# A decoder layer on eight cores: an own buffer for V's last columns, an fp16 copy of w_down made in DRAM, and the first block sums ahead of the LayerNorm statistics

## The chip, the cores and the metric

The kernel runs on all 8 cores of one Trainium2 chip, each core on 2048 of 16384 tokens. The time is that of the slowest core, in microseconds (us) on the device. Each execution of such a program is in one of two states: fast, or slow, where the cores of one die (0 to 3 or 4 to 7), or of both, are granted a lower TensorE clock. The engines are PE (TensorE, matmuls), DVE (VectorE), ACT (ScalarE), POOL (GpSimd) and SP (SyncE, which here only issues transfers). DMA transfers are issued from POOL's queue (q0 in the profile, which can also cast) and from SP's (q1).

## The reference, cut to what matters

```python
proj = x @ w_in + b_in                       # q, k, v of two attention groups
y = concat(rms_norm(group A), rms_norm(group B)) @ w_out
x = layer_norm(ALPHA * x + y, ln1)
gate, up = split(x @ w_up)
x = layer_norm(ALPHA * x + (silu(gate) * up) @ w_down, ln2)   # 2048 -> 5632 -> 2048
```

## The kernel before: the parts that matter

A core first computes K and V for eight tiles of 512 tokens (its own four and the four before them, for the attention window), then attention, the output projection, and SwiGLU. SwiGLU runs twice (`st` = 0, 1: 1024 tokens each), each time with the hidden width in two halves (`g`), with seven block products in place of eight; the operands of the seven are "block sums" made on VectorE.

A scheduler records every operation with the buffers it reads and writes, and puts semaphore waits between them **in program order**. A DMA with `joins=` adds itself to a buffer's writers, and whoever reads the buffer waits for all writers recorded so far.

```python
    for kc in range(KC):                                       # 16 chunks: POOL's queue
        S_.dma("pool", s0[:, kc, :], k.xT_d[0, :, kc, :], [], [b_], ...)          # x, tile 0
        S_.dma("pool", wv[:, kc, 0:1024], k.wv_d[kc, :, 0:1024], [], [bwv[kc]], ...)
    S_.dma("sp", bv, k.bv_d, [bwv[11]], [bbv], "bv")
    load_x(1, (2, 2, 4, 4, 4))
    for h in range(8):
        S_.dma("pool", wk[h], k.wk_d[h], [], [bwk[h]], ...)
    for q in range(4):                                         # V's last 128 columns
        S_.dma("pool", wv[:, 4 * q:4 * q + 4, 1024:1152], ..., [], [], "wvb",
               joins=bwv[4 * q:4 * q + 4])
    ...
    for kc in range(KC):                                       # V of tile 0
        S_.pe(mm, [bx[0][kc], bwv[kc]], k.bBK)
    ...
    for t in range(2, 8):                                      # the other token tiles
        if t >= 3: kb_tile(t)
        for blk in range(4): v_tile(t, blk); flush()           # 2 output buffers, stored by SP
        for h in range(8): k_tile(t, h)                        # 3 output buffers, stored by SP
```

A V tile stores 128 rows of 2304 bytes (2048 in tiles 0 to 2), a K tile 128 rows of 1024 bytes. The down projection loads each block of w_down as fp32, cast to fp16 on the way, once for each `st`; between its blocks it stores and reloads partial results (`z2s`, `x1s`).

The softmax here doesn't subtract the row's maximum and nothing guards it: scores larger than these inputs give would overflow.

## Time and profile before

| | before |
|---|---|
| timed runs, at first | 3138.67 to 3421.52 us, median of 3: 3149.82 |
| profiled run | 2991.6 us, mean granted clock 0.98 on all cores |
| PE's first matmul / first K matmul | 92.83 / 155.56 us |
| token tiles 3 to 7 (267 to 573 us) | PE busy 304.9 of 306 us |
| PE idle in the four down projections | 41 us |

The page of before: busy time by engine, then busy tenths in 40 slices of the span, for PE and the DMA engines.

```profile
PE 2756.5 (92%) x14966; PEld 1324.0 (44%) x15077; DVE 1965.6 (66%) x2700; ACT 735.6 (25%) x1075; POOL 554.9 (19%) x579
...
PE   0799999999999799989999999997899999999995
...
DMA  9745311457665755869977745578588678544653
```

PE is the bound; only the places where its row is below 9 can be won. The first is the start. PE's timeline (start, duration, engine, line, operation, count, and the idle time before with what ended it):

```profile
92.83 30.73 PE L526 MATMUL sp<-arena 128*128 128x512 bf16 x126 [92.83 <-DMA arena<-wv]
126.40 29.32 PE L538 MATMUL sp<-arena 128*128 128x512 bf16 x125 [2.84 <-DVE arena L450]
155.56 4.70 PE L481 MATMUL sp<-arena 128*128 128x512 bf16 x21
```

L526 and L538 are V of tiles 0 and 1, L481 is K. The others show in the list of PE's waits (us in total, times, longest):

```profile
PE sp L526 <- DMA arena<-wv: 92.8, 1, 92.8
PE sp L1382 <- DVE arena L1555: 19.9, 8, 5.8
PE sp L1382 <- DVE arena L1557: 19.6, 6, 8.5
PE sp L1382 <- ACT arena L1510: 14.9, 2, 7.4
```

L1555 and L1557 add reloaded partial results in the down projection; L1510 stands in the first gate/up block of each `st`, behind two LayerNorm tiles on ACT. The stage windows (stretch, length, busy time of each engine, granted clock, DMA share, GB/s) for token tiles 3 to 7, the first down projection, and the second half's first block:

```profile
267.00:573.00 306.00, 304.90 (x1603) 158.55 (x1621) 155.17 (x229) 3.12 (x5) 4.54 (x9) 1.00 0.33 82
1556.00:1700.00 144.00, 133.98 (x610) 59.79 (x609) 83.65 (x106) 0.57 (x1) 4.24 (x8) 0.98 0.81 183
...
2110.00:2160.00 50.00, 40.82 (x174) 17.77 (x172) 33.59 (x41) 11.89 (x17) 10.96 (x10) 0.93 0.52 135
```

In the first row DMA is a third busy and PE has no gap. DMA issues (KB each, median us from issue to landing):

```profile
arena<-wdn POOLq DMA_DIRECT2D x32, 1408.0 KB, 14.7
z2s<-arena SPq DMA_DIRECT2D x48, 512.0 KB, 12.2
...
ka<-arena SPq DMA_DIRECT2D x64, 128.0 KB, 1.7
```

### The profile page before, as it was taken

The page shows a single profiled execution, that of the slowest core. Times are in us where ns is not written, and L with a number is a line of the kernel's source. Part 1 is how long each engine was busy: PE and PEld are TensorE (multiplying, and loading weights), DVE is VectorE, ACT ScalarE, POOL GpSimd, SP SyncE. Part 2 cuts the span into 40 slices and gives each one's busy share as a digit, 9 for nine tenths or more (in the row PEclk, how much of TensorE's full clock was granted, in tenths as well). Part 3 has the DMA queues.
Part 4 walks back from the last instruction along what each step waited for, and adds up shares of the span by engine and source line. Part 5 has one row for each costly group of instructions (what it writes and reads, how often), then busy time and mean ns, then how long its engine had stood idle before and what let it go on. Part 6 is the DMA issues. An engine that isn't in the chain of part 4 may idle for free.

```text
span 2990.6 us, 41458 instructions; the slowest of 8 cores (2976.1 to 2990.6 us)
## 1 busy us (share of the span) xinstructions
PE 2756.5 (92%) x14966; PEld 1324.0 (44%) x15077; DVE 1965.6 (66%) x2700; ACT 735.6 (25%) x1075; POOL 554.9 (19%) x579
## 2 busy tenths in 40 slices
PE   0799999999999799989999999997899999999995
PEld 0344555444566444434444444443344444444442
DVE  0164554588788754478865566675788756666787
ACT  0000000177665424523310022211233200122114
POOL 4000000022111174711100000035200000000167
PEclk9999999999999899999999999999999999999997
DMA  9745311457665755869977745578588678544653
GB/s 158 126 94 114 87 52 50 101 113 130 134 145 121 205 164 155 225 109 152 152 129 181 178 88 91 95 155 216 138 172 171 126 173 184 112 87 89 145 128 116
DMA packets 192570, 400.59 MB, mean 134 GB/s; under 512 B 89072, under 2 KB 112752, under 8 KB 174704
## 3 DMA queue, kind: packets, MB, share of 16 engines
q0 software_dynamic: 36032, 186.43, 38.1%
q1 hardware_dynamic: 142512, 186.32, 22.1%
q10 hardware_dynamic: 13824, 25.17, 2.7%
q8 instruction: 123, 2.02, 0.3%
q14 instruction: 79, 0.65, 0.1%
HBM read 491.42 MB, written 97.06 MB: 197 GB/s over the span
## 4 chain that ended last, share of the span: by engine, by line
PE 78%; DMA 7%; DVE 4%; another core or an unknown queue 3%; issue 3%; ACT 2%; SPq 1%; POOL 1%; ACTq 0%; DVEq 0%; POOLq 0%
PE sp L1382 47%; PE sp L481 7%; PE sp L728 7%; PE sp L468 6%; PE sp L1194 4%; DMA z2s<-arena 4%; SPq L139 1%; DMA arena<-x1s 1%; PE sp L526 1%; PE sp L538 1%; DMA arena<-z2s 1%; PE sp L770 1%; DVE arena L1288 1%; ACT arena L358 1%
## 5 line engine op out<-in xcount | busy, mean ns | idle before, releaser
L1382 PE MATMUL sp<-arena 128*128 128x512 f16 x7408 | 1615.4, 381 | 57.8 <-DVE arena L1555 19.9
L1382 PEld LDWEIGHTS sp<-arena 128*128 128x128 f16 x7408 | 726.3, 98 | 947.5 <-issue 86.5
L1475 DVE TENSOR_TENSOR arena<-sp,arena 128x512 f32<-128x512 f32 (+1 forms) x348 | 236.9, 689 | 175.3 <-PE sp L1382 154.9
L1557 DVE TENSOR_TENSOR arena<-arena,sp 128x512 f32<-128x512 f32 x256 | 166.7, 682 | 131.1 <-PE sp L1382 102.8
L1194 PE MATMUL sp<-arena 128*128 128x512 bf16 x1003 | 224.5, 384 | 10.0 <-DMA arena<-wob 6.9
L728 PE MATMUL sp<-arena 128*128 128x512 bf16 x976 | 226.9, 381 | 5.4 <-ACT arena L358 2.3
L450 DVE TENSOR_TENSOR arena<-sp,arena 128x384 bf16<-128x384 f32 (+1 forms) x81 | 47.8, 605 | 272.5 <-PE sp L526 111.3
L481 PE MATMUL sp<-arena 128*128 128x512 bf16 x1001 | 220.1, 379 | 1.2
L139 POOL DMA_DIRECT2D arena<-wup x88 | 47.0, 535 | 840.2 <-DVE arena L1395 576.7
L1403 DVE TENSOR_TENSOR arena<-arena 128x2048 f16<-128x2048 f16 (+1 forms) x118 | 191.3, 1621 | 0.0
L468 PE MATMUL sp<-arena 128*128 128x384 bf16 (+1 forms) x1036 | 182.4, 337 | 0.4
L1238 POOL TENSOR_TENSOR arena<-arena 128x512 f32<-128x512 f32 x120 | 168.4, 1403 | 25.0 <-ACT arena L1236 22.5
L1237 POOL TENSOR_TENSOR arena<-arena 128x512 f32<-128x512 f32 x120 | 159.1, 1326 | 56.1 <-DVE arena L1557 30.0
L358 ACT ACTIVATE arena<-sp,arena 128x512 bf16<-128x512 f32 (+1 forms) x37 | 24.7, 667 | 575.1 <-PE sp L501 499.8
L1194 PEld LDWEIGHTS sp<-arena 128*128 128x128 bf16 x1024 | 101.1, 99 | 134.0 <-issue 16.7
L1508 ACT ACTIVATE arena<-sp 128x512 f32<-128x512 f32 x86 | 51.4, 597 | 440.1 <-PE sp L1382 439.0
L1236 ACT ACTIVATE arena<-arena 128x512 f32<-128x512 f32 x120 | 75.6, 630 | 332.1 <-DVE arena L1557 170.9
L1395 DVE TENSOR_TENSOR arena<-arena 128x2048 f16<-128x2048 f16 (+1 forms) x118 | 156.3, 1324 | 0.7 <-DMA arena<-wdn 0.6
L1475 DVE TENSOR_TENSOR arena<-arena 128x512 f16<-128x512 f32 (+1 forms) x304 | 154.7, 567 | 0.0
L481 PEld LDWEIGHTS sp<-arena 128*128 128x128 bf16 x1024 | 100.2, 98 | 120.2
L728 PEld LDWEIGHTS sp<-arena 128*128 128x128 bf16 x1024 | 97.7, 98 | 116.2 <-issue 6.4
L468 PEld LDWEIGHTS sp<-arena 128*128 128x128 bf16 x1040 | 101.7, 98 | 79.6
(131 smaller groups left out, 2474.5 us busy)
## 6 DMA issues: line engine op xcount, KB each, us to landing
arena<-wup POOLq DMA_DIRECT2D x88, 1024.0 KB, 10.0
arena<-wdn POOLq DMA_DIRECT2D x32, 1408.0 KB, 14.7
z2s<-arena SPq DMA_DIRECT2D x48, 512.0 KB, 12.2
arena<-xres SPq DMA_DIRECT2D x32, 512.0 KB, 7.6
arena<-wob SPq DMA_DIRECT2D x32, 512.0 KB, 6.8
x1s<-arena ACTq DMA_DIRECT2D x64, 256.0 KB, 6.4
arena<-x1s SPq DMA_DIRECT2D x32, 512.0 KB, 7.3
arena<-z2s SPq DMA_DIRECT2D x32, 512.0 KB, 9.0
```

The costliest lines, as they stand in the source:

```text
L139: return self._add(q, lambda: eng.dma_start(out=out, in_=in_), reads, writes, joins, semkey=semkey)
L468: ins = nc.tensor.matmul(bank(k, bk)[:, 0:c1 - c0], x[:, kc, blk * 128:blk * 128 + 128], wv[:, kc, c0:c1], start=(kc == 0), stop=(kc == KC ...
L481: ins = nc.tensor.matmul(bank(k, bk), wk[h][:, kc, :], x[:, kc, :], start=(kc == 0), stop=(kc == KC - 1))
L728: ins = nc.tensor.matmul(bank(k, bk), w[:, kc, :], x[:, kc, :], start=(kc == 0), stop=(kc == KC - 1))
L1194: ins = nc.tensor.matmul(bank(k, bk), w[:, kc, :], y[:, kc, hh * 512:(hh + 1) * 512], start=(first and i == 0), stop=(last and i == len(kc ...
L1237: S_.pool(lambda: nc.gpsimd.tensor_tensor(out=za, in0=za, in1=z, op=ALU.add), [bz, bza], [bza])
L1238: S_.pool(lambda: nc.gpsimd.tensor_tensor(out=qa, in0=qa, in1=sq, op=ALU.add), [bsq, bqa], [bqa])
L1382: ins = nc.tensor.matmul(bank(k, bk), w, x, start=(first and i == 0), stop=(last and i == len(ws) - 1), skip_group_check=True)
L1395: S_.dve(lambda: nc.vector.tensor_tensor(out=v, in0=w[:, 0:n, :], in1=w[:, n:2 * n, :], op=ALU.add), [bw], [b])
L1403: S_.dve(lambda: nc.vector.tensor_tensor(out=v, in0=w[:, :, 0:128], in1=w[:, :, 128:256], op=ALU.subtract), [bw], [b])
L1475: S_.dve(lambda: nc.vector.tensor_tensor(out=o, in0=a, in1=b, op=op), [ba, bb], [bo])
L1557: S_.dve(lambda: nc.vector.tensor_tensor(out=v, in0=v, in1=o, op=op), [b, bo], [b])
```

## The change

Its intent has three parts. (a) V's last columns get their own buffer, so tile 0 need not wait for them. (b) While PE projects token tiles 3 to 6, 16 DMAs copy w_down to fp16 in DRAM, so that its 32 later loads read half the bytes and need no cast. (c) The sums for PE's next products are made before the statistics, and two LayerNorm tiles leave the first block.

```diff
+    bwvb = Buf("wvb")
@@
-               joins=bwv[4 * q:4 * q + 4])
+               joins=[bwvb])
@@ def v_tile
-            S_.pe(mm, bx[t] + bwv, [k.bBK[bk]])
+            S_.pe(mm, bx[t] + bwv + ([bwvb] if c1 > 1024 else []), [k.bBK[bk]])
@@ for t in range(2, 8)
         for h in range(8):
+            if 3 <= t < 7 and h % 2 == 0:
+                i = (t - 3) * 4 + h // 2
+                k.bwdh[i] = Buf("wdh%d" % i)
+                S_.dma("pool", k.wdh_d[i // 2, i % 2], k.wdn_d[i // 2, i % 2].rearrange("p a j m -> p (a j m)"), [], [k.bwdh[i]], "wdh")
             k_tile(t, h)
@@ loads of w_down: from k.wdh_d[p, g], after k.bwdh[...], in place of k.wdn_d[p, g]
@@ first gate/up block
                         if i == 1:
+                            x_sums(((G3, B21, B11, ALU.subtract),))
+                            u_sums(st, f + 1, "P")
                             while fins:
                                 fins.pop(0)()
...  (the other sums follow one by one)
-                    run_jobs(2)
-                    run_acts()
```

## The prediction

> **What bounds the kernel.** TensorE: the page gives PE 92% busy, and the chain of waits is 78% PE. Only PE's idle stretches can be won. Timeline, stage windows and PE's waits show three kinds:
>
> 1. Start: PE's first matmul (L526) starts at 92.83 us, released by a wv load. By the code, V's last-column loads join the buffers of V's main columns and precede the matmuls in program order, so the first matmul waits for a load queued behind x0, wv, x1 and wk. But bv, which waits for the twelfth wv chunk, was issued at 39.3 us, and ropeA, which waits for the end of x1, at 63.8: tile 0's operands are there near 50 us, tile 1's near 64.
> 2. Down projection: PE waits for VectorE, which waits for x1s/z2s reloads behind z2s stores. The windows show 134.0 of 144, 125.3 of 143, 134.1 of 144 and 134.5 of 138 us busy: 41 us idle, and some 2 us at half rate (0.43 us a matmul, not 0.22) after each gap over 5 us, as in the Trainium skill (TensorE: Matmul & The Clock Gate, What's actually happening). DMA share is 0.81 to 0.85 in the first three.
> 3. First gate/up block of each half: PE waits 0.92 and 1.74 us for VectorE L1395, then 7.43 and 7.45 us for ScalarE L1510, queued behind two LayerNorm tiles, then runs slowly for some 2 us.
>
> **What the change does.**
> (a) Tile 0 of V is paced by its loads and ends near 50 us, not 123. Not all 73 us are won: the V stores stand behind ropeA (63.8 us) on SP's queue and there are two V output buffers, so blocks 2 and 3 free their banks only near 75 us; tile 1's second half ends near 90, when wk has landed too. The first K matmul (L481) moves from 155.5 to about 91 us: 64 us won, all on the critical path, kept by the PE-bound rest.
> (b) Sixteen fp32-to-fp16 copies, 23 MB written. At the software queue's 163 GB/s (186.4 MB in 38.1% of the span; estimate) each takes 9 us of all engines: 140 to 190 us in one burst from about 205 us, where DMA share is 0.1 to 0.9. K stores (1.7 us) will slow to maybe 10; three output buffers and eight banks cover it: cost 0 to 8 us. Later the 32 wdn loads need half the read and no cast: 1.44 MB at q1's 282 GB/s (estimate) is 5 us, not 9, per 16.7 us block. Of 45 us (41 idle plus cold matmuls) I expect 24 back.
> (c) The first G3 and P sums precede the statistics, and no LayerNorm tile stands before L1508/L1510: 20 us in two halves.
>
> Sum: 64 + 24 + 20 - 4 = about 105 us.
>
> **The time.** Before's profiled run took 2991.6 us (fast state); its timed runs, 3138 to 3421, are slow by the 1.5% rule. The change should come to about 2886 in fast runs (ratio 0.965); timed like before, mostly slow, 3150 - 105 = about 3042. The range must hold both: 2870 to 3085. Faster by over 2%: 0.87; within 2%: 0.11; slower: 0.02.
>
> **What would show it.** First L526 before 15 us, first L481 at 85 to 100 us; PE without gaps from 100 to 500 us though DMA share is near 1 from 205 to about 380; w_down loads landing in under 10 us (14.7 before); PE's waits on L1555/L1557 falling from 39.5 to under 20 us; no 7.4 us wait on L1510.
>
> **What would make it wrong.** Copies to DRAM much slower than loads, stalling K and V stores or the x and wq loads; HBM shared by all cores setting the pace in the start; reload waits staying because store latency, not w_down, sets them; timed runs in another state than before's.

## The result, and the profile after

The change made the kernel slower. In the first measurement it took 3228.26 us (median of 4, 3223.96 to 3514.29) against 3145.28 for before (median of 4): ratio 1.0263, 95% interval 1.0218 to 1.0309. Ratios in this text are the mean time of one kernel's fast runs over that of the other's of the same rounds, so not quite the ratio of the medians. The predicted ratio was 0.965, and the measured time lies above the predicted range of 2870 to 3085 us.

That profile fell in the slow state (mean clock 0.90 to 0.93). The same kernel was therefore run again; in the call f2_after all four of its runs and all seven of before were fast, and the ratio was 1.0224 (1.0208 to 1.0239; medians 3062.63 and 2995.99). All lines of "after" are from that profile, taken in the same state as before's. Its page:

```profile
PE 2764.1 (90%) x15077; PEld 1323.3 (43%) x15077; DVE 1981.4 (65%) x2700; ACT 735.6 (24%) x1075; POOL 562.6 (18%) x595
...
PE   6895118999999989999999999999999999999995
...
DMA  9949993124576574476886675446867756554523
```

PE's zero at the start is gone, and so are the later 7s and 8s but one. But there is a new hole, "5118", from slice 4 on, and under it DMA is at 9. PE's timeline at the start (L529 is before's L526, L541 its L538, L484 its L481):

```profile
11.30 5.20 PE L529 MATMUL sp<-arena 128*128 128x512 bf16 x16 [11.30 <-DMA arena<-wv]
...
57.91 15.66 PE L541 MATMUL sp<-arena 128*128 128x512 bf16 x64 [2.91 <-DVE arena L453]
89.89 15.52 PE L541 MATMUL sp<-arena 128*128 128x512 bf16 x64 [16.32 <-DVE arena L453]
105.25 15.06 PE L484 MATMUL sp<-arena 128*128 128x512 bf16 x69
```

So part (a) works: K starts at 105 us, not 155.6. PE's waits:

```profile
PE sp L471 <- DVE arena L344: 134.1, 4, 76.2
PE sp L484 <- DVE arena L453: 31.7, 1, 31.7
...
PE sp L1389 <- DVE arena L1565: 8.5, 6, 3.3
...
PE sp L1389 <- DVE arena L1563: 3.4, 3, 1.5
```

The down projection's waits (L1563 and L1565, before's L1555 and L1557) fell from 39.5 to 11.9 us, and the ACT wait is gone. But PE now waits 166 us in the projections for VectorE to empty its banks. The window from tile 3's start shows how bad it is:

```profile
214.00:467.00 253.00, 87.54 (x411) 41.56 (x409) 33.27 (x50) 1.05 (x2) 11.67 (x23) 0.67 0.99 121
```

PE is busy 88 of 253 us. VectorE is not the cause: it is busy 33 us. Its timeline names what it waits for (L347 writes a K tile's output buffer):

```profile
391.11 0.69 DVE L347 TENSOR_TENSOR arena<-arena 128x512 bf16<-128x512 f32 x1 [84.11 <-DMA ka<-arena]
...
415.12 0.69 DVE L347 TENSOR_TENSOR arena<-arena 128x512 bf16<-128x512 f32 x1 [21.01 <-DMA ka<-arena]
...
441.02 0.69 DVE L347 TENSOR_TENSOR arena<-arena 128x512 bf16<-128x512 f32 x1 [22.90 <-DMA ka<-arena]
...
464.27 0.69 DVE L347 TENSOR_TENSOR arena<-arena 128x512 bf16<-128x512 f32 x1 [20.24 <-DMA ka<-arena]
```

One K store is done every 23 to 26 us, where PE makes a K tile every 3.45 us. The DMA view of the same stretch (225 to 430 us), packets and bytes by queue:

```profile
q0 software_dynamic: 1534, 22.67, 96.9%
q1 hardware_dynamic: 1533, 2.65, 4.4%
...
ka<-arena SPq DMA_DIRECT2D x5, 128.0 KB, 92.6
```

**1534 packets of POOL's queue (the copies, and until about 248 us the x loads ahead of them) and 1533 of SP's (the stores, and two loads of rotary tables between them).** Here the two queues take turns, one packet each; but the turns of POOL's queue take 97% of the engines' time and those of SP's 4%. Over the whole execution:

```profile
arena<-wdh POOLq DMA_DIRECT2D x32, 1408.0 KB, 8.2
z2s<-arena SPq DMA_DIRECT2D x48, 512.0 KB, 7.2
wdh<-wdn POOLq DMA_DIRECT2D x16, 1408.0 KB, 145.7
```

The later loads got what was intended (14.7 to 8.2 us, the z2s stores 12.2 to 7.2). The copies landed 46 to 241 us after issue: one queue, one burst. The first, issued at 218.5 us, landed 46.4 us later; the last, issued at 225.9 us, 241.3 us later. So one landed every 13.5 us ((467.2 - 264.9) / 15).

### The profile page after: what moved, and what is told of

It is laid out like the page before. It is cut to its first block, busy times and chain, and to the rows that moved or that the text cites. A ratio compares the mean times of both kernels' runs of the same rounds, so it can differ in the third digit from the quotient of the medians.

```text
span 3222.9 us, 41604 instructions; the slowest of 8 cores (3139.9 to 3222.9 us)
## 1 busy us (share of the span) xinstructions
PE 2952.4 (92%) x15077; PEld 1368.3 (42%) x15077; DVE 1987.2 (62%) x2700; ACT 735.5 (23%) x1075; POOL 557.1 (17%) x595
## 3 DMA queue, kind: packets, MB, share of 16 engines
q0 software_dynamic: 37312, 209.50, 36.5%
## 4 chain that ended last, share of the span: by engine, by line
PE 84%; another core or an unknown queue 6%; DMA 3%; DVE 2%; issue 2%; SPq 1%; ACT 1%; POOL 1%; DVEq 0%; ACTq 0%; POOLq 0%
PE sp L1389 54%; PE sp L1201 7%; PE sp L735 6%; PE sp L484 6%; PE sp L471 4%; DMA vs<-arena 1%; DMA arena<-xT 1%; SPq L139 1%; POOL arena L139 1%; PE sp L541 1%; PE sp L777 1%; DVE arena L1650 1%; ACT arena L359 0%; DMA ys<-arena 0%
## 5 line engine op out<-in xcount | busy, mean ns | idle before, releaser
L1389 PE MATMUL sp<-arena 128*128 128x512 f16 x7408 | 1783.2, 409 | 4.9 <-DVE arena L1565 1.9
L1389 PEld LDWEIGHTS sp<-arena 128*128 128x128 f16 x7408 | 767.1, 104 | 1021.3 <-issue 600.8
L471 PE MATMUL sp<-arena 128*128 128x384 bf16 (+1 forms) x1040 | 192.1, 348 | 134.0 <-DVE arena L344 133.6
L1565 DVE TENSOR_TENSOR arena<-arena,sp 128x512 f32<-128x512 f32 x256 | 167.6, 683 | 169.2 <-PE sp L1389 168.5
L484 PE MATMUL sp<-arena 128*128 128x512 bf16 x1024 | 224.0, 381 | 28.5 <-DVE arena L453 28.5
L1201 PE MATMUL sp<-arena 128*128 128x512 bf16 x1024 | 232.5, 392 | 2.3 <-DMA arena<-wob 2.3
L735 PE MATMUL sp<-arena 128*128 128x512 bf16 x1024 | 233.9, 381 | 0.0
L1410 DVE TENSOR_TENSOR arena<-arena 128x2048 f16<-128x2048 f16 (+1 forms) x118 | 202.2, 1713 | 0.0
L471 PEld LDWEIGHTS sp<-arena 128*128 128x128 bf16 x1040 | 104.1, 101 | 220.8 <-issue 145.2
L347 DVE TENSOR_TENSOR arena<-arena 128x512 bf16<-128x512 f32 x96 | 77.9, 812 | 181.4 <-DMA ka<-arena 168.8
L484 PEld LDWEIGHTS sp<-arena 128*128 128x128 bf16 x1024 | 100.5, 98 | 150.4 <-issue 31.6
L1201 PEld LDWEIGHTS sp<-arena 128*128 128x128 bf16 x1024 | 102.6, 100 | 132.5 <-issue 33.8
L1402 DVE TENSOR_TENSOR arena<-arena 128x2048 f16<-128x2048 f16 (+1 forms) x118 | 157.4, 1334 | 0.0
```

The lines of the kernel that those rows point to most:

```text
L471: ins = nc.tensor.matmul(bank(k, bk)[:, 0:c1 - c0], x[:, kc, blk * 128:blk * 128 + 128], wv[:, kc, c0:c1], start=(kc == 0), stop=(kc == KC ...
L484: ins = nc.tensor.matmul(bank(k, bk), wk[h][:, kc, :], x[:, kc, :], start=(kc == 0), stop=(kc == KC - 1))
L735: ins = nc.tensor.matmul(bank(k, bk), w[:, kc, :], x[:, kc, :], start=(kc == 0), stop=(kc == KC - 1))
L1201: ins = nc.tensor.matmul(bank(k, bk), w[:, kc, :], y[:, kc, hh * 512:(hh + 1) * 512], start=(first and i == 0), stop=(last and i == len(kc ...
L1389: ins = nc.tensor.matmul(bank(k, bk), w, x, start=(first and i == 0), stop=(last and i == len(ws) - 1), skip_group_check=True)
L1402: S_.dve(lambda: nc.vector.tensor_tensor(out=v, in0=w[:, 0:n, :], in1=w[:, n:2 * n, :], op=ALU.add), [bw], [b])
```

## The experiments

Theory A: the burst of copies starves the K and V stores, and the rest of the change works. Within it, A1: a store is held because each of its packets waits for one packet of a copy; A2: the copies use up the engines or the DRAM, whatever their packets. Rival B: the denser kernel is granted a lower clock, and that ate the gain.

| run | what it is | ratio to before (95%) | us against before | PE busy, 214 to 514 us |
|---|---|---|---|---|
| f2_after | the change | 1.0224 (1.0208 to 1.0239) | +67 | 132 of 300 |
| e1_no_copy | the change without the copies | 0.9751 (0.9734 to 0.9769) | -75 | 300 |
| e4_copy_only | the copies alone | 1.0451 (1.0426 to 1.0476) | +135 | other times |
| e2_short_runs | the change, copies in runs of 352 elements | 0.969 (0.9654 to 0.9725) | -93 | 300 |
| e5_half_rows | the change, copies in half rows | 0.9843 (0.9698 to 0.9988) | noisy | 223 |
| e3_paced | the change, copies spread | 0.9684 (0.9665 to 0.9703) | -95 | 288 |
| e8_paced_half | e3, in half rows | 0.9668 (0.9648 to 0.9689) | -99 | 289 |
| e9_more_v_out | e8, more V output buffers | 0.966 (0.964 to 0.968) | -102 | other times |
| e6b_own_buffer | part (a) alone | 0.9821 (0.9802 to 0.984) | -54 | - |
| e7_early_sums | part (c) alone | 0.9854 (0.9767 to 0.9942) | noisy | - |

"Us against before" is (ratio - 1) times the median of before: 2996.68 for e1 to e4, 2995.99 for f2, e6b, e8 and e9. The call with e5, e6, e7 and f1 was disturbed: of its 11 runs of before 8 were slow, and even the fast ones went from 3018.83 to 3046.79. There only the traces are used, not the ratios. e6 is not in the table: it has no ratio, and e6b repeats it. e1 to e4 ran on chip 7 and all later runs on chip 0 (f1's expectation below says the chip of the first four, which is not so); the medians of before, 2996.68 and 2995.99, agree.

### Taking the copies away, and the copies alone

e1 takes the copies out of the changed kernel; e4 puts them alone into the kernel before, as the change has them.

```diff
# e1, against the change
-                S_.dma("pool", k.wdh_d[i // 2, i % 2], k.wdn_d[i // 2, i % 2]..., [], [k.bwdh[i]], "wdh")
-  (("d", st, g, p), k.wdh_d[p, g]...)          # loads of w_down
+  (("d", st, g, p), k.wdn_d[p, g]...)
```

> The changed kernel with w_down's copy undone (own buffer for V's last columns and early block sums stay). Theory A (the burst of 16 DRAM-to-DRAM copies starves the K and V stores, so the projections stop; the rest of the change works): no PE gap over 5 us between 110 us and the end of the projections, where the changed kernel had 253 - 91 = 162 us idle from 214 to 467 us; first K matmul L484 near 103 us as there (155.5 before); down-projection waits as before (about 40 us); time ratio to before 0.970 to 0.982 (52 + 20 us of 3143 won). Rival B (the chip grants a lower clock as the kernel gets denser, and that ate the gain, not the copies): ratio 0.995 or more, with a mean clock below that of before's runs in the same rounds by about as much.

> The kernel before with the fp16 copy of w_down alone, issued in one burst as in the change. Theory A: PE idles 140 to 185 us in token tiles 3 to 5, the down projection gets back about 40 us, ratio to before 1.030 to 1.045. Rival B: the loss is not in the copies: ratio under 1.01.

The stage windows of e1 and of e4:

```profile
214.00:514.00 300.00, 300.00 (x1606) 156.21 (x1604) 150.57 (x222) 3.12 (x5) 4.78 (x9) 1.00 0.34 82
```

```profile
267.00:573.00 306.00, 137.81 (x659) 66.80 (x657) 63.22 (x96) 1.37 (x2) 10.68 (x22) 0.72 0.89 118
```

e1 won 75 us and PE had no gap from 214 to 514 us; e4 lost 135 us and PE was busy 137.8 of the 306 us from 267 to 573 us, where it was busy 304.9 before. Both are as theory A expected, e4's ratio at the upper edge of its range. B falls: e1's mean clock was 0.98, as before's, and it was faster. e4's mean clock was 0.96, but in that window, where PE stands idle, it was 0.72 against before's 1.00; 0.28 less for 306 of 3140 us makes 0.03, which covers the lower mean. The two parts add up: -75 + 135 = +60, against +67 measured for the whole, where each of the three has an interval of some 5 to 8 us.

The clock bears on one thing only: the first measurement's times lie 5% above the later ones. The change's two fast runs there had mean clocks of 0.90, against 0.96 in f2. Before's first timed runs have no recorded clock, so that they shared it is likely and not shown.

### Why the copies starve the stores: shorter runs

```diff
# e2, against the change: the same bytes in the same burst, in runs of 352 elements
-  S_.dma("pool", k.wdh_d[i // 2, i % 2], k.wdn_d[i // 2, i % 2].rearrange("p a j m -> p (a j m)"), ...)
+  S_.dma("pool", k.wdh_d[i // 2, i % 2].rearrange("p (c e) -> c p e", c=16),
+         k.wdn_d[i // 2, i % 2].rearrange("p a j m -> p (a j m)").rearrange("p (c e) -> c p e", c=16), ...)
```

> The changed kernel with each copy issued over runs of 352 elements (1408 bytes read, 704 written) in place of whole 5632-element rows; same bytes, same burst. Theory A1 (a store's eight 1 KB packets per DMA engine each wait for one packet of a copy, about 18 KB written or 2.4 us, so a K store takes 20 us): the copies' packets shrink to about 6 KB written (230 packets a copy, not 80), a K store in the burst takes 6 to 10 us instead of 20 and more, PE's idle time in the burst falls from 162 us to 20 to 70 us, ratio to before 0.975 to 1.0. Rival A2 (the DMA engines' or DRAM's rate is used up by the copies, whatever their packets): K stores stay at 20 us and more, idle stays at 140 us or more, ratio about 1.02.

The DMA view of e2 from 235 to 400 us, and its window from 214 to 514 us:

```profile
q0 software_dynamic: 18918, 14.97, 86.7%
q1 hardware_dynamic: 5981, 9.36, 20.2%
...
ka<-arena SPq DMA_DIRECT2D x23, 128.0 KB, 8.2
```

```profile
214.00:514.00 300.00, 300.00 (x1606) 156.34 (x1605) 150.13 (x222) 3.12 (x5) 21.24 (x25) 1.00 1.05 147
```

PE is full for 300 us with the DMA engines at a share of 1.05, more than in the change (0.99). Full DMA engines did not stop PE, so A2 falls. For A1 this run is support, not proof. One expectation was off: I thought that several runs would share a packet (230 packets a copy). The queue's totals give (69056 - 36032) / 16 = 2064 a copy, one for each of the 2048 runs and 16 more. And the counts are not one for one here: 18918 to 5981, though SP's queue had more than one transfer in flight on average (23 K stores of 8.2 us and nine V stores of 9.3 us make 272 us in these 165 us). By turns of one such packet a K store would be held about 1.3 us (165 us x 16 engines / 18918, nine times); it took 8.2 us. The expected 6 to 10 us had been worked out from 230 packets, so that hit was luck, or the engine's turns hold several of the packets that the profile counts; no run here tells which.

Two things keep e2 from being the best form. The copies ran slower (POOL was held between issues, and the last copy was issued at 406.7 us, not 225.9), and DMA stayed full to about 530 us. So the wq loads behind the copies came late, and PE lost 14 us at the start of attention. Besides, e2 changes the pace of issue along with the packets, though its queue stayed deep: seven copies were issued by 226 us, and each later one 0.3 us after one had landed. The next run keeps the burst.

### A dose in between: half rows

```diff
# e5, against the change: two DMAs a copy, half a row each
-  S_.dma("pool", k.wdh_d[i // 2, i % 2], k.wdn_d[i // 2, i % 2]..., [], [k.bwdh[i]], "wdh")
+  for z in range(2):
+      S_.dma("pool", k.wdh_d[i // 2, i % 2, :, z * 2816:z * 2816 + 2816],
+             k.wdn_d[i // 2, i % 2]...[:, z * 2816:z * 2816 + 2816], [], [], "wdh", joins=[k.bwdh[i]])
```

> The changed kernel with every copy cut into two transfers of half rows (2816 elements, 11 KB read and 5.6 KB written a run), issued in the same burst. Theory A1 (a store waits for one copy packet per packet of its own): if the packets follow the runs, a K store in the burst takes between the 8 us of 0.7 KB runs and the 20 us and more of whole rows, 10 to 15 us, and PE's idle time lies between 0 and 162 us, I expect 20 to 80; ratio 0.97 to 1.0. If the packets stay at 18 KB, store times and idle time stay as with whole rows.

All 32 DMAs were issued at once (215 to 231 us) and the DMA engines were full, as in the change. Queues of e5 from 300 to 360 us, then VectorE's waits for K's output buffers:

```profile
q0 software_dynamic: 1189, 5.95, 90.1%
q1 hardware_dynamic: 1193, 1.65, 10.3%
```

```profile
298.98 0.69 DVE L347 TENSOR_TENSOR arena<-arena 128x512 bf16<-128x512 f32 x1 [4.96 <-DMA ka<-arena]
...
305.27 0.69 DVE L347 TENSOR_TENSOR arena<-arena 128x512 bf16<-128x512 f32 x1 [3.29 <-DMA ka<-arena]
...
312.51 0.69 DVE L347 TENSOR_TENSOR arena<-arena 128x512 bf16<-128x512 f32 x1 [4.23 <-DMA ka<-arena]
```

Again one for one, and a K store is now done every 6.3 to 7.2 us. The packets account for both rates. The queue's totals give 80 packets for a whole-row copy ((37312 - 36032) / 16, where 36032 are before's) and 144 for a half-row DMA ((40640 - 36032) / 32). The packet records of the traces show what is in them: 16 of each have 4 bytes, which I take for the engines' completion messages; the other 64 of a whole-row copy have 22528 bytes each, two whole rows as written, and took 3.3 us in the mean; the other 128 of a half-row DMA have 5632 bytes, one half row, and took 0.81 us. A K store, by the same count, has 128 + 16 packets (an estimate: it has 128 rows). On each of the 16 engines:

| | packets a DMA, per engine | one DMA lands every (last landing less first) | per packet (mean) | 9 packets of a K store (estimate) | measured between K stores |
|---|---|---|---|---|---|
| whole rows | 5 | 13.5 us | 2.70 us | 24.3 us | 23.3 to 25.9 us |
| half rows | 9 | 7.27 us ((480.4 - 255.0) / 31) | 0.81 us | 7.3 us | 6.3 to 7.2 us |

Two doses, two rates; the first estimate is met, the second is high by some 8% (the two intervals shown have a mean of 6.8 us). A K tile takes PE 3.45 us. So even half rows starve it, only less: 77 us idle, not 168, in the 300 us from 214 us. The expected range of idle time (20 to 80 us) held, but a K store's time from issue to landing was 20.8 us, not 10 to 15: several stores stand in one queue, and each waits for those ahead of it as well.

### The same copies, spread

```diff
# e3, against the change: each copy waits for a V or K store of its tile
+    def copy_wd(i, after):
+        S_.dma("pool", k.wdh_d[i // 2, i % 2], k.wdn_d[i // 2, i % 2]..., [after], [k.bwdh[i]], "wdh")
@@ after v_tile(t, blk), blk 0 and 2
+                copy_wd((t - 3) * 4 + blk // 2, k.bvs[-1])
@@ after k_tile(t, h), h 1 and 5
+                copy_wd((t - 3) * 4 + 2 + h // 4, k.bka[h][-1])
```

> The changed kernel with its 16 copies spread: each waits for a V or K store of the token tile it stands in, two in the V part and two in the K part of each of four tiles of 62 us. Theory A: one copy at a time (about 12 us at the 118 GB/s of the burst), stores late by at most one copy, PE idle in the projections under 15 us, down-projection waits under 8 us as in the changed kernel, ratio to before 0.955 to 0.970. Rival B: ratio 0.985 or more, lower clock. Rival A2: idle of 60 us or more in tiles 3 to 6.

```profile
214.00:514.00 300.00, 287.99 (x1535) 149.79 (x1533) 131.63 (x200) 3.12 (x5) 12.78 (x25) 0.99 0.88 141
```

PE idles 12 us in the 300, the time is 95 us below before, and the clock 0.98: theory A on all counts but a small one. PE's down-projection waits were 15.1 us (11.0 + 4.1), not under 8. With the same whole rows and one or two copies in the queue, K stores still take 13.1 us in the median, but between copies they catch up (from 310 to 316 us, for instance, no packet with copy data was on the engines), and then three output buffers and eight banks are enough.

e8 cuts each paced copy into half rows.

> As e3 (paced), with each copy cut into two half-row transfers. By the one-for-one turn of packets (1510 copy packets against 1510 store packets in the whole-row burst, 3170 against 3057 in the half-row burst) a store meeting a copy is held half as long: K stores 6 to 9 us in the median instead of 13, PE idle in token tiles 3 to 6 under 5 us instead of 12, ratio 0.962 to 0.968. If stores are held by the copies' bytes and not by their packets, nothing changes: K stores 13 us, idle 12 us, 0.968.

This missed: K stores 12.5 us, idle time 10.6 us, ratio within e3's interval. The turns themselves did not fail: from 300 to 318 us the trace has 385 packets of POOL's queue and 387 of SP's. So with paced copies it hardly mattered how they were cut; why the store time didn't fall further is open.

### The other parts, each alone

e6 is part (a) on the kernel before, e7 part (c).

> The kernel before with the own buffer for V's last columns alone. First V matmul at 10 to 13 us, first K matmul L482 at 100 to 107 us in place of 155.5, PE full from there: 46 to 57 us won, ratio 0.981 to 0.986.

> The kernel before with the early block sums alone (first sums ahead of the statistics, no LayerNorm tiles in the first block). The waits of 7.4 us on ScalarE and 0.9 and 1.7 us on VectorE at the start of each half are gone: 15 to 24 us won, ratio 0.992 to 0.995, clear of noise with five rounds.

> The own buffer alone again, for the same reason: 40 to 57 us won, 0.981 to 0.987 in fast runs.

e6b won 54 us; its first K matmul came at 105.6 us, as in the change. e7's trace shows the effect: in the second half's first block, where PE had been busy 40.82 of 50 us, it is now

```profile
2110.00:2160.00 50.00, 50.00 (x231) 22.50 (x230) 45.32 (x63) 17.67 (x26) 2.16 (x4) 1.00 0.60 119
```

(core 6, whose mean clock of 0.985 is that of undisturbed runs). (c) is the difference of e1 and e6b: 75 - 54 = 21 us, with some 8 us either way from the two intervals, which come from two calls. e6's trace agrees with e6b's: its first K matmul came at 102.6 us.

The change itself was first rerun in the disturbed call, and gave no usable interval (1.0111, 0.9958 to 1.0265), with PE's waits as in f2 (133.3 and 27.8 us in the projections). The second rerun is the one quoted above.

> The changed kernel itself, unedited, on the chip that ran the first four experiments. If its parts add up, its distance to before is that of the copies alone (e4: +135 us of 2997) and that of the rest (e1: -75 us), +60 us, ratio 1.015 to 1.027 in fast runs, PE idle 150 to 175 us between the third token tile's start and the end of the burst. Rival: on the first chip part of the loss was its lower granted clock (0.90 in its profile, 0.98 in before's); then here the ratio falls below 1.01.

> The changed kernel again, since its run on the noisy chip had no usable interval: 1.015 to 1.027 in fast runs, as the sum of e1 (-75 us) and e4 (+135 us).

### A try at the start

The start still loses time: tile 1's second half waits 16 us for banks (timeline above), because V stores under the load burst take 14.3 us in the median and there are two output buffers. e9 lends four rotary buffers to V in tiles 0 and 1.

```diff
# e9, against e8
-        vi = nx("vo", 2)
-        vo, bvo = VO[vi]
+        vi = nx("vo", 2 if t >= 2 else 6)
+        vo, bvo = VO[vi] if vi < 2 else (T1 + T2)[vi - 2]
+        if vi >= 2:
+            vo = vo.bitcast(BF16)
```

> Paced half-row copies (as e8) and, in token tiles 0 and 1, four more V output buffers, lent by the rotary buffers that no K tile needs yet. If the start still loses what the prediction left out because V stores of 8.9 to 20.5 us hold two output buffers, then tile 1's second half starts at 60 to 66 us instead of 86, the first K matmul at 76 to 85 us instead of 103, and the ratio is 15 to 27 us below e8's: 0.952 to 0.961. Rival: the loads set the start (wk lands too late): first K matmul waits for wk, near 90 us or later.

PE's timeline:

```profile
87.48 51.96 PE L486 MATMUL sp<-arena 128*128 128x512 bf16 x240
...
146.80 5.16 PE L473 MATMUL sp<-arena 128*128 128x512 bf16 x16 [3.42 <-DVE arena L344]
...
160.65 5.06 PE L473 MATMUL sp<-arena 128*128 128x512 bf16 x16 [4.14 <-DVE arena L344]
```

The gap is gone and K starts at 87.5 us, 17.8 earlier than e8's 105.2, without waiting for wk; but the ratio is within e8's interval. Both missed the expectation (76 to 85 us for K's start, 0.952 to 0.961 for the ratio). K's stores now fall into the burst of x loads, and PE waits for K's output buffers in place of V's: of the 97 us from 103 to 200 it is busy 87, where e8's is busy 97. When tile 3 starts, 3.9 us of the 17.8 are left. The gain became a new wait of the same kind.

## Why the prediction was right or wrong

**Where it failed.** The step was, as the prediction put it: "K stores (1.7 us) will slow to maybe 10; three output buffers and eight banks cover it: cost 0 to 8 us." A K store every 23 to 26 us was the fact, PE idled about 168 of 300 us, and the copies alone cost 135 us net of what they won later. Two errors lie in that sentence.

- It took the store's time for a delay that buffers hide. Stores of one queue beside the burst came one after another: what matters is the time *between* two landings. At 10 us between stores the three buffers would have been used up after a few tiles too, since a K tile takes 3.45 us. Buffers cover a short burst; they don't cover a rate that is too low for over 200 us. K stores got through the x loads of before, which the prediction does not mention, but that was such a short burst (4.2 MB in some 30 us, a K store in it took 13.0 us).
- It costed the copies by bytes and looked for free DMA time. The burst fits into the projections' idle DMA time, more or less (DMA full from about 216 us, with x loads first, to 467; I had said 205 to 380). But in both bursts the engine was shared by packets, and the size of the copies' packets set a store's rate. The Trainium skill (DMA: Bandwidth & Descriptors, Queues, rings and completion order) says that each DMA engine goes round the queues "at *packet* granularity". The prediction did not draw on it. The traces of the two bursts agree with it nearly to a packet, 1534 to 1533 and 1189 to 1193; e2's, 18918 to 5981, does not, if the profile's packets are the page's.

I also read the program order as a schedule: the diff puts a copy before every second K tile, but nothing makes a copy wait, so POOL issued all 16 within 8 us. The prediction said so ("in one burst") and saw no harm in it.

**Where it was right in kind and off in size.**

- Start: 64 us predicted, 54 measured (e6b). The mechanism held, to the banks of blocks 2 and 3. The term mis-sized is V's stores, which were to be through in time for banks to be free near 75 us; a median of 14.3 us put the second half of tile 1 at 89.9 us and K at 105.
- Copies: 9 us each predicted from the load queue's 163 GB/s, 13.5 measured.
- Down projection: waits from 39.5 to under 20 us predicted, 11.9 measured; loads under 10 us predicted, 8.2 measured. Net of what stays lost in the projections, the paced copies are worth 20 to 24 us (e3 and e8 against e1, e8 from another call); the sum had 24 - 4. The prediction's "some 2 us at half rate" is what is lost and not how long it lasts: after before's five gaps over 5 us from 1300 us on, 7 to 11 matmuls took 0.43 us each, 3.0 to 4.7 us.
- First block: 20 us predicted, 21 measured, some 8 either way (e1 less e6b).

Without the failed step the sum was sound: 105 us predicted, 95 and 99 measured for the change with its copies spread (e3, e8). As for the absolute time, the prediction expected runs like before's first ones and hedged for fast ones; the state was not what broke it, since the ratio is 1.02 to 1.03 in both calls.

## What to carry to other kernels

When a background transfer is put into a stage with small stores on another queue, count packets, not bytes: time between stores = packets of the store on one engine x mean time of one packet of the transfer, and compare that with the rate at which the stage makes outputs. (This is worked out from two deep bursts, of packets of 22528 and 5632 bytes; with runs of 704 bytes, e2, and with paced copies, e8, it did not give the store's time.) Buffers hide a burst, never a rate that is too low. A DMA without a dependency is issued as soon as its queue takes it, wherever it stands in the program (all 16 copies within 8 us): make a long series wait for something that keeps pace with the stage, or cut it into short runs.

## What the Trainium skill lacked or had wrong

- DMA: Bandwidth & Descriptors, Queues, rings and completion order, has the turn by packets, which the two bursts confirm (1534 packets to 1533), but not what it does to a small transfer: K stores of 128 KB landed 23 to 26 us apart beside whole-row copies and 6.3 to 7.2 us apart beside half-row copies, with the DMA engines full in both. It calls packets of 9 to 17 descriptors typical. If its packets are the profile's, the copies here had one short run, one half row or two whole rows a packet (2064 packets for 2048 runs, 144 for 128 half rows, 80 for 128 rows, 16 of each being completions).
- The same page, Rules for kernel authors, advises to coalesce small transfers into large ones. Its rules do not say what the long runs of a large transfer do to another queue's stores: here each copy was one DMA of 1408 KB both times, and runs of 352 elements left PE full (300 of 300 us), whole rows left it 132.
- The same page, Anatomy of one DMA, fits a transfer as 2.0 us plus bytes at 436 GB/s, which is 8.6 us for the 2.88 MB that a copy reads (an estimate from the page). A casting copy from DRAM to DRAM took 13.5 us in a row of 16, on all 8 cores at once. No page that I read has a figure for a copy from DRAM to DRAM that casts; for copies without a cast between DRAM tensors there is one.
- TensorE: Matmul & The Clock Gate, Seeing it yourself, tells all-core kernels to budget 13/16 of the clock for dense matmuls. Here 8 cores running matmuls 95% of the time had a mean granted clock of 0.98 in fast runs (e1, e8); values near 13/16 (0.80 to 0.83) were seen only on the slow die of the slowest runs (e4, e7, f1 and the change's first call). The page gives this for its default power profile; which profile this chip has is not on record.
